# Merge and branch products of a hybrid diffusion layer: token halves as the standing operand, 512 weight columns as the moving one

## The chip, the cores and the metric

One NeuronCore of one Trainium2 chip. The metric is device time of one execution in microseconds, lower is better. Engines: TensorE (PE, with weight loads PEld), VectorE (DVE), ScalarE (ACT), GpSimd (POOL) and SyncE (SP), which here issues all DMA.

## What is computed

One layer over 256 latent tokens (D = 2048) with 256 context tokens. After modulation and a first RMSNorm, one input projection feeds two mixers and two gates; the part at issue is the merge that follows them:

```
y   = sigmoid(gate_a) * (att @ w_branch_attn) + sigmoid(gate_r) * (rec @ w_branch_rec)
x   = x + g1 * (y @ w_out)
x   = x + g2 * conv_ffn(modulate(x, norm2_w, sh2, sc2), ...)
out = rms_norm(x, final_norm_w)
```

`gate_a` and `gate_r` (256 x 2048 each) are the last 4096 columns of the input projection `h @ w_in`. `att` (256 x 1024) is the differential attention's result. `rec = rms_norm(o, w) * silu(g)` (256 x 1024) is that of a bidirectional gated recurrence over 8 heads. All is float32.

## The kernel before

**Precision.** A float32 product is made of three products in a rounded format (fp32r): each operand is split into a high part and the rest, and high x high, high x rest and rest x high are added in PSUM. An activation is kept as a pair [high, rest]; a weight is split when it comes in.

**Weights.** `stage()` (line 65) loads a unit of 128 partitions x 1024 floats into `raw` (4 buffers), ScalarE copies it to `whi`, VectorE subtracts to `wlo` (3 buffers each). `gemm2` (line 132) lets a 128 x 128 weight tile stand and the tokens pass: one matmul of 512 columns (high and rest of 256 tokens) against the high weight, one of 256 columns against the low weight. The result, channels on partitions, has two halves in PSUM, which `fold()` (line 141) adds: a ScalarE copy and a VectorE addition. The earlier input tiles with context go through `gemm` (line 110), three matmuls of 512.

**Background.** The modulation's remaining columns (64 tiles x 2 halves, "wm") are loaded by `background()` into the same `raw` buffers and consumed by VectorE (line 345). One is taken from the list every so many ticks: each weight unit of `gemm2` is one tick, of `gemm` two, and `bg_rate` gives loads a tick: 0.5 and 0.7 in the attention, 0.1 in the recurrence, 0.55 in the merge and after. A load is consumed when the next one is issued. At the recurrence's begin all but 64 are issued.

**Flows.** Attention heads and recurrence heads are generators that a tick moves on, so that their small matmuls and transposes stand between weight units. In the recurrence one flow runs at a time (`depth[0] = 1`).

**Order.** First stage (to about 145 us): modulation and norm, with the first seven input tiles. Attention (to about 412). Recurrence (to about 800): at each head, projections, their preparation on all engines, then `start(head(...))`. At head 0 the gates of channel tiles 0 and 1 follow (8 units). Then 8 tiles of the output gate `RG`, the rest of the flows, and `rec`.

**Merge.** For each of 16 channel tiles j: the two gates of tile j + 2 (4 units, PSUM from `acc`, 3 banks), the attention branch (1 unit) and the recurrence branch (1 unit, PSUM `macc`, 4 banks), each with a fold. GpSimd multiplies gates, VectorE multiplies and adds, and ScalarE and VectorE split `y` into its pair (lines 720 and 721). The recurrence's row statistic `rrstd` is a 128 x 256 tile, equal on all partitions.

**Output projection.** 16 tiles of 2 units; tiles 0 and 1 interleave, first the units with y tiles 0 to 7, then those with 8 to 15. The residual follows each tile.

**Planner.** The Tile framework orders each engine's instructions ahead of time, from the program's order as a priority and its own costs; so an instruction can stand far from its place in the program. Weight splits have a raised priority. Buffers of one tag rotate; a load waits until its buffer is let go.

Of the kernel before, what the change touches and what calls it, by code (L numbers as in the profile page):

```python
# [8 lines left out]
F32 = mybir.dt.float32  # L9
# [15 lines left out]
GROUP0 = [AK, AV, AK + 1, AV + 1, RFF, RFB, RI]  # L25
NB = 10
C1 = 3
# [13 lines left out]
@with_exitstack  # L41
def body(ctx, tc, cst_d, sel_d, cb_d, ccol_d, wn_d, xT_d, xc_d, lam_d, rope_d, mask_d, wm_d, wg0_d, win_d, wba_d,
         wbr_d, wout_d, wu0_d, wup_d, wdn_d, out_d):
    nc = tc.nc
# [87 lines left out]
    def gemm2(tiles_, xs):  # L132
# [6 lines left out]
        assert all(k == len(xs) for k in ks)  # L139

    def fold(dst, ps):
        act.copy(dst, ps[:, :T])
        dve.tensor_add(dst, dst, ps[:, T:])
# [4 lines left out]
    sel = cpool.tile([P, 2], F32, name="sel")  # L148
    cb = [big.tile([P, 1024], F32, tag="x1", name=f"cb{i}", bufs=4) for i in range(2)]

# [4 lines left out]
    with ExitStack() as es:  # L155
# [139 lines left out]

        sg = big.tile([P, 1024], F32, tag="x1", name="sg", bufs=4)
        for i in range(2):
# [23 lines left out]

    def gates(j, dst):
        for i, base in enumerate((GA, GR)):
            ps = in_tile(base + j)
            fold(dst[:, i], ps)
            act.activation(dst[:, i], dst[:, i], AF.Sigmoid)
        return [dst[:, 0], dst[:, 1]]

    bg = [(t, half) for half in range(2) for t in range(32, 96)]

    with ExitStack() as esa:
# [19 lines left out]
        with ExitStack() as es:  # L351
# [5 lines left out]
            ls = at.tile([P, 6], F32, name="ls")  # L357
            lj = at.tile([P, 64], F32, name="lj")
            lamt = at.tile([P, 256], F32, name="lamt")
            dma.dma_start(lamt, lam_d)  # L360
            for i in range(2):
# [19 lines left out]
            def head(h, kT, vr, qT):  # L381
# [60 lines left out]
                pe.matmul(ops[:, 1], ones, osq, start=True, stop=True)  # L442
                rs = at.tile([P, 2, T], F32, tag="rs", name="rs")
                act.activation(rs[:, 0], ops[:, 1], AF.Sqrt, bias=epst, scale=1.0 / P)
                dve.reciprocal(rs[:, 1], rs[:, 0])
                dve.scalar_tensor_tensor(o, o, subw, rs[:, 1], op0=ALU.mult, op1=ALU.mult)
                a = big.tile([P, 2, T], F32R, tag="ar", name=f"att{h}", bufs=16)
# [37 lines left out]

        rraw = [big.tile([P, 4, T], F32, tag="x1", name=f"rraw{i}", bufs=4) for i in range(2)]
        rrstd = cpool.tile([P, T], F32, name="rrstd")
        with ExitStack() as es:
# [29 lines left out]
            def head(h, kkq, kc, PL, PC, vr):  # L518
# [35 lines left out]

                yield 1
                tp = rps.tile([P, 4, P], F32, tag="aux", name="tp", bufs=2)
# [56 lines left out]
            background(max(0, len(bg) - 64))  # L613
            g01 = big.tile([P, 2, 2, T], F32, tag="x1", name="g01", bufs=4)
            depth[0] = 1
            bg_rate[0] = BG_REC
            for h in range(8):
# [53 lines left out]
            act.activation(rrstd, s2, AF.Sqrt, bias=epst, scale=1.0 / 1024)  # L671
            dve.reciprocal(rrstd, rrstd)
# [17 lines left out]
    def residual_load(i):  # L690
        t_ = big.tile([P, 4, T], F32, tag="x1", name=f"x1_{i}", bufs=4)
        dma.dma_start(t_, xT_d[:, 4 * i:4 * i + 4])
        x1.append(t_)
# [4 lines left out]

    residual_load(0)
    residual_load(1)  # L700
    bg_rate[0] = BG_MRG
    y = []
    for j in range(KT):
        gs = pre[j]
        if j + 2 < KT:
            pre.append(gates(j + 2, et.tile([P, 2, T], F32, tag="gate", name="gate", bufs=3)))
        pa = acc5()
        gemm2([(pa, [(wba_d[j], 1024)])], att)
        t1 = et.tile([P, T], F32, tag="e2", name="t1", bufs=4)
        fold(t1, pa)  # L710
        pool.tensor_tensor(gs[0], t1, gs[0], ALU.mult)
        pool.tensor_tensor(gs[1], rrstd, gs[1], ALU.mult)
        pr = acc5()
        gemm2([(pr, [(wbr_d[j], 1024)])], rec)
        t2 = et.tile([P, T], F32, tag="e2", name="t2", bufs=4)
        fold(t2, pr)
        dve.tensor_mul(t2, t2, gs[1])
        dve.tensor_add(t2, t2, gs[0])
        yy = et.tile([P, 2, T], F32R, tag="y", name=f"y{j}", bufs=16)
        act.copy(yy[:, 0], t2)  # L720
        dve.tensor_sub(yy[:, 1], t2, yy[:, 0].bitcast(F32))
        y.append(yy)

# [27 lines left out]
    mod_sum(32, 48)  # L751
    residual_load(2)
    sqs = et.tile([P, T], F32, tag="sqs", name="sqs2")
# [58 lines left out]
    for j in range(FT):  # L812
# [35 lines left out]
        else:  # L848
            fj = et.tile([P, 2, T], F32R, tag="y", name=f"f{j}", bufs=16)
        act.copy(fj[:, 0], sg)  # L850
# [32 lines left out]

_INS = ["cst", "sel", "cb", "ccol", "wn", "xT", "xc", "lam", "rope", "mask", "wm", "wg0", "win", "wba", "wbr", "wout", "wu0", "wup", "wdn"]


def _layout(np, x, c, ctx, c_ctx, w_mod, b_mod, norm1_w, w_in, lam_q1, lam_k1, lam_q2, lam_k2, subln_w, rec_lb,
# [10 lines left out]
    def halves(w):  # L898
        t = tiles(w)
        return np.ascontiguousarray(t.reshape(t.shape[0], P, 2, 1024).transpose(0, 2, 1, 3))  # L900

    lam = np.concatenate([A["lam_q1"][0], A["lam_k1"][0], A["lam_q2"][0], A["lam_k2"][0]])
# [13 lines left out]
    def tok(a):  # L916
# [21 lines left out]
               xc=np.concatenate([tok(A["x"]), tok(A["ctx"])], axis=2), lam=np.broadcast_to(lam, (P, 256)), rope=rope, mask=mask, wm=wm, wg0=g0,  # L938
               win=halves(wi), wba=tiles(A["w_branch_attn"][0]), wbr=tiles(A["w_branch_rec"][0]),
               wout=halves(A["w_out"][0]), wup=halves(A["w_up"][0]), wdn=tiles(A["w_down"][0]))  # L940
# [21 lines left out]
```

## Time and profile before

| | |
|---|---|
| three runs, us | 1902.01, 1905.36, 1903.25 (median 1903.25) |
| the profiled execution, us | 1907.5, its span 1905.7 |
| mean granted TensorE clock | 0.993 of full speed |
| busy share: PE, PEld, DVE, ACT, POOL | 97%, 82%, 71%, 52%, 19% |

The span is from the first to the last instruction of the profiled execution; the runs are timed without a profile. Busy shares are means over stages with different limits. A matmul's duration in the profile is its passage through a pipeline; what it costs in a stream is the distance from its start to the next one's.

### The profile page before, as it was taken

Reading aid. Unit: us, or ns where it says so; the run is one execution under the profiler, and the core shown is the slowest. Engines: PE = TensorE matmul, PEld = TensorE weight load, DVE = VectorE, ACT = ScalarE, POOL = GpSimd, SP = SyncE. Lnnn points to the kernel's source line nnn. Section 1 sums busy time; section 2 is a strip of 40 time slices with the busy share of each in tenths; the row PEclk is TensorE's granted clock in tenths of the full one; section 3 lists DMA queues with packets and bytes.
Section 4 is the critical chain, followed back from the end, with each engine's and each line's share of the span. In section 5 each row is a group of like instructions: output and inputs, shape, how many; then the busy total and the mean of one; then the engine's idle time right before and its main releaser. Section 6 shows DMA issues by size and latency. Waiting matters only on the chain.

```text
span 1905.7 us, 27947 instructions
## 1 busy us (share of the span) xinstructions
PE 1846.0 (97%) x10430; PEld 1559.7 (82%) x10430; DVE 1359.8 (71%) x2130; ACT 996.9 (52%) x1503; POOL 367.6 (19%) x328
## 2 busy tenths in 40 slices
PE   7999999998999999999999999999999999999997
PEld 3777778777788888888888789888888888888886
DVE  4449888888866667977877879776777767644444
ACT  3336455447655556744444556655555555544342
POOL 0002100003232333410110120322223222211111
PEclk9999999999999999999999999999999999999999
DMA  9977666684233333688888866666666666666664
GB/s 375 362 272 231 205 198 205 211 274 133 78 110 111 114 108 113 209 271 279 274 271 272 266 190 181 189 192 189 188 193 189 193 188 188 188 188 189 193 192 123
DMA packets 112360, 385.71 MB, mean 202 GB/s; under 512 B 12384, under 2 KB 16608, under 8 KB 112224
## 3 DMA queue, kind: packets, MB, share of 16 engines
q1 hardware_dynamic: 112224, 383.92, 63.5%
q8 instruction: 82, 1.34, 0.3%
q14 instruction: 54, 0.44, 0.1%
HBM read 381.78 MB, written 2.10 MB: 201 GB/s over the span
## 4 chain that ended last, share of the span: by engine, by line
PE 63%; DMA 9%; DVE 8%; issue 3%; ACT 2%; POOL 0%; DVEq 0%; ACTq 0%; POOLq 0%
PE macc L126 28%; PE macc L127 15%; DMA raw<-in_wm 9%; PE acc L126 5%; PE acc L77 3%; PE acc L78 3%; PE acc L79 3%; DVE wlo L73 3%; PE acc L127 2%; DVE raw L345 1%; PE lv L590 1%; ACT whi L72 1%; DMA raw<-in_win 0%; DVE PL L643 0%; PE stp L581 0%
## 5 line engine op out<-in xcount | busy, mean ns | idle before, releaser
L73 DVE TENSOR_TENSOR wlo<-raw,whi 128x1024 fp32r<-128x1024 f32 (+1 forms) x514 | 630.6, 1227 | 247.9 <-ACT whi L72 242.1
L72 ACT CAST whi<-raw 128x1024 fp32r<-128x1024 f32 (+1 forms) x514 | 530.3, 1033 | 443.4 <-PE macc L126 162.0
L126 PE MATMUL macc<-h,whi 128*128 128x512 f32 x1344 | 466.0, 391 | 0.0
L127 PE MATMUL macc<-h,wlo 128*128 128x256 f32 x1344 | 376.3, 280 | 0.0
L126 PE MATMUL acc<-h,whi 128*128 128x512 f32 x896 | 321.6, 400 | 0.0
L126 PEld LDWEIGHTS macc<-h,whi 128*128 128x128 f32 x1344 | 251.3, 187 | 55.1
L127 PE MATMUL acc<-h,wlo 128*128 128x256 f32 x896 | 253.7, 283 | 4.9 <-DVE wlo L73 4.7
L127 PEld LDWEIGHTS macc<-h,wlo 128*128 128x128 f32 x1344 | 254.0, 189 | 0.0
L126 PE MATMUL macc<-f,whi 128*128 128x512 f32 x704 | 244.1, 391 | 0.0
L77 PE MATMUL acc<-h,whi 128*128 128x512 f32 x528 | 211.4, 400 | 0.0
L79 PE MATMUL acc<-h,wlo 128*128 128x512 f32 x528 | 207.0, 392 | 0.7 <-DVE wlo L73 0.7
L78 PE MATMUL acc<-h,whi 128*128 128x512 f32 x528 | 207.3, 393 | 0.0
L345 DVE SCALAR_TENSOR_TENSOR raw<-raw,cb 128x1024 f32<-128x1024 f32 x128 | 162.7, 1272 | 61.8 <-DMA raw<-in_wm 61.4
L126 PEld LDWEIGHTS acc<-h,whi 128*128 128x128 f32 x896 | 169.3, 189 | 37.5 <-ACT whi L72 0.4
L127 PE MATMUL macc<-f,wlo 128*128 128x256 f32 x704 | 197.1, 280 | 0.0
L127 PEld LDWEIGHTS acc<-h,wlo 128*128 128x128 f32 x896 | 170.1, 190 | 11.5 <-DVE wlo L73 11.1
L126 PEld LDWEIGHTS macc<-f,whi 128*128 128x128 f32 x704 | 131.6, 187 | 28.9
L127 PEld LDWEIGHTS macc<-f,wlo 128*128 128x128 f32 x704 | 133.1, 189 | 0.0
L842 POOL TENSOR_TENSOR u<-u 128x256 f32<-128x256 f32 x44 | 69.3, 1574 | 327.9 <-DVE u L837 287.9
L79 PEld LDWEIGHTS acc<-h,wlo 128*128 128x128 f32 x528 | 99.3, 188 | 22.4 <-DVE wlo L73 1.2
L78 PEld LDWEIGHTS acc<-h,whi 128*128 128x128 f32 x528 | 99.6, 189 | 21.5 <-issue 2.8
L77 PEld LDWEIGHTS acc<-h,whi 128*128 128x128 f32 x528 | 99.4, 188 | 21.2 <-issue 2.3
(740 smaller groups left out, 2639.3 us busy)
## 6 DMA issues: line engine op xcount, KB each, us to landing
raw<-in_win SPq DMA_DIRECT2D x178, 512.0 KB, 4.2
raw<-in_wup SPq DMA_DIRECT2D x168, 512.0 KB, 3.5
raw<-in_wm SPq DMA_DIRECT2D x128, 512.0 KB, 4.4
raw<-in_wdn SPq DMA_DIRECT2D x80, 512.0 KB, 3.7
nraw<-in_wn SPq DMA_DIRECT2D x64, 512.0 KB, 7.2
raw<-in_wout SPq DMA_DIRECT2D x32, 512.0 KB, 3.6
raw<-in_wba SPq DMA_DIRECT2D x16, 512.0 KB, 4.6
raw<-in_wbr SPq DMA_DIRECT2D x16, 512.0 KB, 4.6
```

The lines of the kernel that those rows point to most:

```text
L72: act.copy(hi[:, :n], raw[:, :n])
L73: dve.tensor_sub(lo[:, :n], raw[:, :n], hi[:, :n].bitcast(F32))
L77: pe.matmul(ps, wh, xh, start=first, stop=False)
L78: pe.matmul(ps, wh, xl, start=False, stop=False)
L79: pe.matmul(ps, wl, xh, start=False, stop=last)
L126: pe.matmul(ps, hi[:, c_], xs[k][:, :, :T], start=k == 0, stop=False)
L127: pe.matmul(ps[:, :T], lo[:, c_], xs[k][:, 0, :T], start=False, stop=k == len(xs) - 1)
L345: dve.scalar_tensor_tensor(raw, raw, 1.0, cb[half], op0=ALU.mult, op1=ALU.mult, accum_out=modp[:, t - 32, half:half + 1])
L590: pe.matmul(lvp[:, m], E[:, 0, m * P:(m + 1) * P], E[:, 1, m * P:(m + 1) * P], start=True, stop=True)
L842: pool.tensor_tensor(cs[1], cs[0], cs[1], ALU.mult)
```

## The change

The gates and both branch products go to a new `gemmx`: halves of the tokens (128 each) stand, 512 weight columns pass, so the result has tokens on partitions and 512 channels in a bank. High and rest add up in the same bank, and `fold` isn't needed. A group g of 512 channels takes 8 units for each gate and 4 for each branch; the weights are laid out for it on the host (`wide`). `rrstd` becomes a column of two numbers per partition. The sums are turned back to channels on partitions by transposes in a flow (`turn`). Both gates of group 0 are made at head 0 of the recurrence (16 units, PSUM from the 3 banks of `acc`), and the attention branch of group 0 right behind the recurrence's flows. The output projection interleaves four tiles at its start. Residual loads stand behind the merge loop. Some buffers change count or tag (`x1` 5, `nraw` 9, the `RG` tile shares `sq`).

```diff
-NB = 10
+NB = 9
...
+    def gemmx(pss, units, xs, k=0):
+        for src in units:
+            hi, lo = stage(src, 1024)
+            for i in range(2):
+                c_ = slice(i * 512, (i + 1) * 512)
+                for m in range(2):
+                    t_ = slice(m * P, (m + 1) * P)
+                    pe.matmul(pss[m], xs[k][:, 0, t_], hi[:, c_], start=k == 0, stop=False)
+                    pe.matmul(pss[m], xs[k][:, 1, t_], hi[:, c_], start=False, stop=False)
+                for m in range(2):
+                    t_ = slice(m * P, (m + 1) * P)
+                    pe.matmul(pss[m], xs[k][:, 0, t_], lo[:, c_], start=False, stop=k == len(xs) - 1)
+                k += 1
+            tick(1)
...
-    def gates(j, dst):
-        for i, base in enumerate((GA, GR)):
-            ps = in_tile(base + j)
-            fold(dst[:, i], ps)
-            act.activation(dst[:, i], dst[:, i], AF.Sigmoid)
-        return [dst[:, 0], dst[:, 1]]
+    def acc3():
+        return acc.tile([P, 512], F32, tag="acc", name="acc")
+
+    def gate(i, g, accs):
+        pss = [accs() for _ in range(2)]
+        gemmx(pss, [wgt_d[i, g, u] for u in range(8)], hx)
+        dst = big.tile([P, 2, 512], F32, tag="x1", name="gate", bufs=5)
+        for m in range(2):
+            act.activation(dst[:, m], pss[m], AF.Sigmoid)
+        return dst
+
+    def branch_att(ga, g, accs):
+        pa = [accs() for _ in range(2)]
+        gemmx(pa, [wbr_d[0, g, u] for u in range(4)], att)
+        for m in range(2):
+            dve.tensor_mul(ga[:, m], pa[m], ga[:, m])
...
-        rrstd = cpool.tile([P, T], F32, name="rrstd")
+        rrstd = cpool.tile([P, 2], F32, name="rrstd")
...
-                yield 1
+                yield 4 if h == 0 else 1
...
-                    pre = [gates(j, g01[:, j]) for j in range(2)]
+                    pre = [gate(i, 0, acc3) for i in range(2)]
...
-                t_ = rt.tile([P, T], F32, tag="rg", name="rg")
+                t_ = rt.tile([P, T], F32, tag="sq", name="rg")
...
             drain()
+            branch_att(pre[0], 0, acc3)
             sp = rps.tile([P, 4, P], F32, tag="aux", name="sp", bufs=2)
-            s2 = sp[:, 0:2].rearrange("p a b -> p (a b)")
-            pe.matmul(s2, ones, sqacc, start=True, stop=False)
-            pe.matmul(s2, ones, sqlast, start=False, stop=True)
+            for m in range(2):
+                t_ = slice(m * P, (m + 1) * P)
+                pe.matmul(sp[:, m, 0:2], sqacc[:, t_], ones[:, 0:2], start=True, stop=False)
+                pe.matmul(sp[:, m, 0:2], sqlast[:, t_], ones[:, 0:2], start=False, stop=True)
...
-    residual_load(0)
-    residual_load(1)
     bg_rate[0] = BG_MRG
     y = []
-    for j in range(KT):
-        gs = pre[j]
-        if j + 2 < KT:
-            pre.append(gates(j + 2, et.tile([P, 2, T], F32, tag="gate", name="gate", bufs=3)))
-        pa = acc5()
-        gemm2([(pa, [(wba_d[j], 1024)])], att)
...
+    def turn(yy, ty):
+        yield 2
+        for m in range(2):
+            t_ = slice(m * P, (m + 1) * P)
+            tp = acc.tile([P, 4, P], F32, tag="acc", name="tp")
+            for i in range(4):
+                pe.transpose(tp[:, i], ty[:, m, i * P:(i + 1) * P], ident)
+            act.copy(yy[:, :, 0, t_], tp)
+            dve.tensor_sub(yy[:, :, 1, t_], tp, yy[:, :, 0, t_].bitcast(F32))
+            yield 1
+
+    for g in range(4):
+        ga, gr = pre if g == 0 else [gate(i, g, acc5) for i in range(2)]
+        if g:
+            branch_att(ga, g, acc5)
+        pr = [acc5() for _ in range(2)]
+        gemmx(pr, [wbr_d[1, g, u] for u in range(4)], rec)
+        for m in range(2):
+            dve.scalar_tensor_tensor(gr[:, m], pr[m], rrstd[:, m:m + 1], gr[:, m], op0=ALU.mult, op1=ALU.mult)
+            dve.tensor_add(gr[:, m], gr[:, m], ga[:, m])
+        yy = et.tile([P, 4, 2, T], F32R, tag="y", name=f"y{g}", bufs=4)
+        start(turn(yy, gr))
+        y += [yy[:, i] for i in range(4)]
+    for i in range(3):
+        residual_load(i)
...
-    residual_load(2)
...
     for j in range(KT):
-        if j % 2 == 0:
-            pair = [(acc5(), [(wout_d[j + i, 0], 1024), (wout_d[j + i, 1], 1024)]) for i in range(2)]
+        if j % 4 == 0:
+            four = [(acc5(), [(wout_d[j + i, 0], 1024), (wout_d[j + i, 1], 1024)]) for i in range(4)]
             if j == 0:
-                gemm2(pair, y)
-        if j > 1:
-            gemm2([pair[j % 2]], y)
-        ps = pair[j % 2][0]
+                gemm2(four, y)
+                drain()
+        if j > 3:
+            gemm2([four[j % 4]], y)
+        ps = four[j % 4][0]
```

## Rows read from the trace of the kernel before

**Rows 1.** The page: busy time, share of the span and instructions of each engine.
```profile
PE 1846.0 (97%) x10430; PEld 1559.7 (82%) x10430; DVE 1359.8 (71%) x2130; ACT 996.9 (52%) x1503; POOL 367.6 (19%) x328
```

**Rows 2.** Busy us (and instructions) by stretch; clock, DMA share, GB/s.
```profile
812.00:1063.00 251.00, 242.83 (x1340) 205.59 (x1339) 194.49 (x276) 116.63 (x185) 26.83 (x29) 0.99 0.84 273
...
1063.00:1080.00 17.00, 14.78 (x76) 12.56 (x75) 15.16 (x26) 7.88 (x11) 0.90 (x2) 0.90 0.83 272
...
1080.00:1100.00 20.00, 20.00 (x117) 17.50 (x116) 17.84 (x30) 11.49 (x23) 4.30 (x4) 1.00 0.78 248
```

**Rows 3.** TensorE's list, eight pairs from start to start (start, duration, line).
```profile
901.00 0.39 PE L126 MATMUL macc<-att,whi 128*128 128x512 f32 x1
...
903.78 0.39 PE L126 MATMUL macc<-rec,whi 128*128 128x512 f32 x1
```

**Rows 4.** TensorE's list: the merge's first gate matmul.
```profile
800.27 0.58 PE L126 MATMUL acc<-h,whi 128*128 128x512 f32 x1
```

**Rows 5.** Line 126: min/median/max ns, first and last start.
```profile
L126 PEld LDWEIGHTS macc<-y,whi x256: 187/188/335, 1063.3 to 1155.8; 128*128 128x128 f32 x128
...
L126 PE MATMUL macc<-y,whi x256: 391/395/796, 1063.4 to 1156.0; 128*128 128x512 f32 x128
```

**Rows 6.** Waits in the merge, SyncE's queue last: us, times, longest.
```profile
PEld acc L127 <- DVE wlo L73: 10.0, 19, 1.1
...
DVE raw L345 <- DMA raw<-in_wm: 30.5, 39, 2.8
...
SPq L341 <- DVE raw L345: 60.2, 32, 4.1
```

**Rows 7.** The chain that ended last, in the merge, shares by line.
```profile
by line: DMA raw<-in_wm 45.8%; issue 14.8%; PE acc L126 8.7%; DVE wlo L73 7.2%; PE macc L126 6.7%; PE acc L127 4.9%; PE macc L127 3.7%; DVE raw L345 2.8%; ACT whi L72 2.5%; DMA raw<-in_wba 1.8%; DVE gate L143 0.7%; DVE t L717 0.6%; DVE t L1
```

**Rows 8.** TensorE's list, a stream of 512-wide matmuls, 21 steps.
```profile
505.67 0.39 PE L79 MATMUL acc<-h,wlo 128*128 128x512 f32 x1
...
510.44 0.39 PE L79 MATMUL acc<-h,wlo 128*128 128x512 f32 x1
```

**Rows 9.** Stretch 812 to 1063: tile raw (VectorE, ScalarE), then line 345 (VectorE).
```profile
812.00:1063.00 251.00, 162.03 (x176) 88.37 (x85) 0.99 0.84 273
...
812.00:1063.00 251.00, 60.08 (x92) 0.99 0.84 273
```

**Rows 10.** Groups of the attention stage: busy us, mean ns of one.
```profile
L415 DVE SCALAR_TENSOR_TENSOR p<-p,z 128x512 f32<-128x512 f32 x16 | 12.1, 753 | 0.1
...
L424 DVE TENSOR_TENSOR aT<-tp,aT 128x512 fp32r<-128x512 f32 x16 | 10.4, 679 | 0.0
...
L423 ACT CAST aT<-tp 128x512 fp32r<-128x512 f32 x16 | 9.4, 587 | 8.5 <-PE tp L421 8.4
```

**Rows 11.** TensorE's list around four transposes.
```profile
420.93 0.60 PE L558 MATMUL tp<-ident,g0sb 128*128 128x128 f32 x4
...
421.29 0.48 PE L126 MATMUL acc<-h,whi 128*128 128x512 f32 x1
```

**Rows 12.** TensorE's waits at the output projection's start.
```profile
PE macc L126 <- DVE y L721: 2.2, 1, 2.2
```

**Rows 13.** ScalarE's list: one table load.
```profile
810.06 1.28 ACT L326 ACT_TABLE_LOAD   x1
```

**Rows 14.** TensorE's waits at heads 0 and 1 of the recurrence.
```profile
PE ktp L565 <- issue: 3.0, 1, 3.0
...
PE ktp L565 <- DVE KQ L526: 2.6, 1, 2.6
```

**Rows 15.** SyncE's waits in the first stage.
```profile
SPq L182 <- PE nat L177: 59.0, 16, 5.0
```

**Rows 16.** SyncE's issues in the merge.
```profile
846.60 0.33 SPq L341 DMA_DIRECT2D raw<-in_wm  x1
...
848.12 0.42 SPq L692 DMA_DIRECT2D x<-in_xT  x1
...
865.09 0.33 SPq L341 DMA_DIRECT2D raw<-in_wm  x1
```

More of the change, by code (lines that the diff above doesn't have):

```diff
@@ L41, in body @@
 @with_exitstack
-def body(ctx, tc, cst_d, sel_d, cb_d, ccol_d, wn_d, xT_d, xc_d, lam_d, rope_d, mask_d, wm_d, wg0_d, win_d, wba_d,
-         wbr_d, wout_d, wu0_d, wup_d, wdn_d, out_d):
+def body(ctx, tc, cst_d, sel_d, cb_d, ccol_d, wn_d, xT_d, xc_d, lam_d, rope_d, mask_d, wm_d, wg0_d, win_d, wgt_d, wbr_d,
+         wout_d, wu0_d, wup_d, wdn_d, out_d):
     nc = tc.nc
@@ L139, in gemm2 @@
         assert all(k == len(xs) for k in ks)
+    def gemmx(pss, units, xs, k=0):
[12 more added lines that the diff above has]
+            tick(1)
+        assert k == len(xs)
     def fold(dst, ps):
@@ L148, in body @@
     sel = cpool.tile([P, 2], F32, name="sel")
-    cb = [big.tile([P, 1024], F32, tag="x1", name=f"cb{i}", bufs=4) for i in range(2)]
+    cb = [big.tile([P, 1024], F32, tag="x1", name=f"cb{i}", bufs=5) for i in range(2)]
     hx = [None] * KT
@@ L294, in body @@
             g0raw[GROUP0[i]] = r
-        sg = big.tile([P, 1024], F32, tag="x1", name="sg", bufs=4)
+        sg = big.tile([P, 1024], F32, tag="x1", name="sg", bufs=5)
         for i in range(2):
@@ L357, in body @@
             ls = at.tile([P, 6], F32, name="ls")
-            lj = at.tile([P, 64], F32, name="lj")
-            lamt = at.tile([P, 256], F32, name="lamt")
-            dma.dma_start(lamt, lam_d)
+            lamt = big.tile([P, 320], F32, tag="ar", name="lamt", bufs=16)
+            lj = lamt[:, 256:]
+            dma.dma_start(lamt[:, :256], lam_d)
             for i in range(2):
@@ L442, in head @@
                 pe.matmul(ops[:, 1], ones, osq, start=True, stop=True)
[L443 to L446, printed above, removed]
+                rs = at.tile([P, T], F32, tag="rs", name="rs")
+                act.activation(rs, ops[:, 1], AF.Sqrt, bias=epst, scale=1.0 / P)
+                dve.reciprocal(rs, rs)
+                dve.scalar_tensor_tensor(o, o, subw, rs, op0=ALU.mult, op1=ALU.mult)
                 a = big.tile([P, 2, T], F32R, tag="ar", name=f"att{h}", bufs=16)
@@ L483, in body @@
             drain()
-        rraw = [big.tile([P, 4, T], F32, tag="x1", name=f"rraw{i}", bufs=4) for i in range(2)]
-        rrstd = cpool.tile([P, T], F32, name="rrstd")
+        rraw = [big.tile([P, 4, T], F32, tag="x1", name=f"rraw{i}", bufs=5) for i in range(2)]
+        rrstd = cpool.tile([P, 2], F32, name="rrstd")
         with ExitStack() as es:
@@ L613, in body @@
             background(max(0, len(bg) - 64))
-            g01 = big.tile([P, 2, 2, T], F32, tag="x1", name="g01", bufs=4)
             depth[0] = 1
@@ L690, in residual_load @@
     def residual_load(i):
-        t_ = big.tile([P, 4, T], F32, tag="x1", name=f"x1_{i}", bufs=4)
+        t_ = big.tile([P, 4, T], F32, tag="x1", name=f"x1_{i}", bufs=5)
         dma.dma_start(t_, xT_d[:, 4 * i:4 * i + 4])
@@ L697, in mod_sum @@
         dve.tensor_add(modv[:, a:b], modv[:, a:b], col("bmod", a, b - a))
-    residual_load(0)
-    residual_load(1)
     bg_rate[0] = BG_MRG
     y = []
-    for j in range(KT):
-        gs = pre[j]
-        if j + 2 < KT:
-            pre.append(gates(j + 2, et.tile([P, 2, T], F32, tag="gate", name="gate", bufs=3)))
-        pa = acc5()
-        gemm2([(pa, [(wba_d[j], 1024)])], att)
[L709 to L722, printed above, removed]
+    def turn(yy, ty):
[22 more added lines that the diff above has]
+        residual_load(i)
     warm = et.tile([P, 1], F32, name="warm")
@@ L848, in body @@
         else:
-            fj = et.tile([P, 2, T], F32R, tag="y", name=f"f{j}", bufs=16)
+            if j % 4 == 0:
+                fp = et.tile([P, 4, 2, T], F32R, tag="y", name=f"f{j}", bufs=4)
+            fj = fp[:, j % 4]
         act.copy(fj[:, 0], sg)
@@ L881, in body @@
             finish(dve, 2, c_)
-_INS = ["cst", "sel", "cb", "ccol", "wn", "xT", "xc", "lam", "rope", "mask", "wm", "wg0", "win", "wba", "wbr", "wout", "wu0", "wup", "wdn"]
+_INS = ["cst", "sel", "cb", "ccol", "wn", "xT", "xc", "lam", "rope", "mask", "wm", "wg0", "win", "wgt", "wbr", "wout", "wu0", "wup", "wdn"]
 def _layout(np, x, c, ctx, c_ctx, w_mod, b_mod, norm1_w, w_in, lam_q1, lam_k1, lam_q2, lam_k2, subln_w, rec_lb,
@@ L900, in halves, with wide @@
         return np.ascontiguousarray(t.reshape(t.shape[0], P, 2, 1024).transpose(0, 2, 1, 3))
+    def wide(w):
+        k, n = w.shape
+        return w.reshape(k // 256, 2, P, n // 512, 512).transpose(3, 0, 2, 1, 4).reshape(n // 512, k // 256, P, 1024)
     lam = np.concatenate([A["lam_q1"][0], A["lam_k1"][0], A["lam_q2"][0], A["lam_k2"][0]])
@@ L938, in _layout @@
                xc=np.concatenate([tok(A["x"]), tok(A["ctx"])], axis=2), lam=np.broadcast_to(lam, (P, 256)), rope=rope, mask=mask, wm=wm, wg0=g0,
-               win=halves(wi), wba=tiles(A["w_branch_attn"][0]), wbr=tiles(A["w_branch_rec"][0]),
+               win=halves(wi[:, :GA * P]),
+               wgt=np.stack([wide(wi[:, b * P:(b + 16) * P]) for b in (GA, GR)]),
+               wbr=np.stack([wide(A["w_branch_attn"][0]), wide(A["w_branch_rec"][0])]),
                wout=halves(A["w_out"][0]), wup=halves(A["w_up"][0]), wdn=tiles(A["w_down"][0]))
```

2 lines of the change are left out of this document (1 added, 1 removed).

## The prediction

> **What bounds the kernel now.** I read the engine line of the page first: TensorE has work for 97% of the span, and VectorE is next with 71% [rows 1]. The busy time by stage then shows where that average hides something: in the merge (812 to 1063 us) VectorE is busy 194 of 251 us and TensorE is not full [rows 2]. So the question is what a weight unit (1024 columns of a weight tile per partition) costs there, against what TensorE alone needs. In a clean stretch of the instruction list a pair of matmuls, 512 and then 256 columns, recurs 8 times in 2.78 us, 0.3475 us each [rows 3]; that is one unit. The merge runs 88 units (14 channel tiles × 2 gates × 2, and 32 for the branches) between its first gate matmul [rows 4] and the first output-projection matmul [rows 5]: 1063.4 − 800.3 = 263.1 us, 2.99 us a unit. So 0.21 us of each unit, 18 us in all, is not TensorE's.
>
> Who takes it? The list of waits says that TensorE stands for the low half of a weight [rows 6], that VectorE stands idle for a modulation transfer (wm) on 39 occasions, and that SyncE holds the next wm load until VectorE has finished the one before. The chain inside the merge runs 45.8% through those transfers [rows 7]. So the four raw buffers set the pace there: a load lands, VectorE consumes it, the buffer goes to the next load.
>
> **The change, part by part.** *The product on TensorE.* Per 256 rows of depth and 512 output channels it was 8 pairs, and is 12 matmuls of 512 columns: the same columns. In a stretch of 512-wide matmuls 21 steps take 4.77 us, 0.227 us each [rows 8], so a unit needs 12 × 0.227 = 2.73 us in place of 2.78. The gain is small, for in the pair the 256-wide one costs 0.3475 − 0.227 = 0.12 us, about half. The Trainium skill, Perfetto Trace Analysis, Optimizing Tensor Performance, says that larger matmuls are more efficient than smaller ones. TensorE: Matmul & The Clock Gate, Back-to-back issue gap, gives about 131 ns for N=512 and 81 ns for N=128 in a stream; an estimate by interpolation from that page, 98 ns for 256, makes 8 pairs 1.83 us and twelve wide ones 1.57 us, 0.26 us a unit instead of 0.05, 25 us over 96 units. The trace doesn't agree: 227 ns [rows 8], not 131.
>
> *Where the units run.* 20 units stand outside the merge loop now (16 for the first two gates, 4 for the first attention branch, beside the recurrence or right behind it, where few wm loads come), 76 inside; it was 8 and 88. Before: 8 × 2.78 + 263.1 = 285.3 us. After: 20 × 2.73 + 76 r. If the raw buffers don't hold TensorE any more, r is 2.73 and the sum 262.1 (−23.2). If they hold it as now, r is 2.99 and the sum 281.8 (−3.5). For the first: the low half is needed after four matmuls (0.91 us), no longer after one (0.23 us), and the waits for it are mostly short; VectorE loses the folds and products, all that it did outside the raw tile, 194.5 − 162.0 = 32.5 us [rows 2, 9], and gets 30 operations of 512 columns at 0.68 to 0.75 us [rows 10], 21 us. ScalarE and GpSimd lose work too. For the second: 39 of 46 times VectorE waited for the transfer itself [rows 6, 9], and a shorter queue on VectorE makes no transfer land sooner. I take the middle, r = 2.86: 54.6 + 217.4 = 272.0, **−13.3 us**.
>
> *Modulation loads pushed on.* 64 are left when the recurrence begins. At 0.1 a tick and 112 ticks, then 0.55 and 88, 4 were left for the output projection; with 124 ticks and then 76, 10 are. Six more stand beside the first residuals, where VectorE is already busy 33.0 of 37 us [rows 2]. At the merge's price, 0.21 × 1.82 units = 0.38 us each, **+2.3**; bounds 0 (hidden) and 6 × 1.31 = 7.8, a full consumption each [rows 9].
>
> *Transposes.* 32 new ones in 8 sets of four. A set of the recurrence takes 0.36 us of TensorE's list [rows 11]: **+2.9**. They stand two and three ticks behind the product, where their sources are long done, save for the last group.
>
> *The boundary to the output projection.* The wait of 2.2 us for the last y [rows 12] goes, since four tiles' first halves (8 to 11 us) need only the first two groups. Late next is the last group's second set: its transposes come three units in, 8.2 us, then a ScalarE copy (0.59) and a VectorE subtraction (0.68) [rows 10] with their queues, against a need after 4 units and 4 pairs, 12.5 us. About a microsecond is left, so **−1.5**, bounds −2.2 and +2.
>
> *PSUM banks of the early gates.* Each holds two of three banks for 8 units; the second gate's second bank waits until the first gate's sigmoid has left it. From rows: the tail of a matmul 0.39 [rows 3], a table load 1.28 [rows 13], a 512-wide ScalarE pass 0.59 [rows 10], less the two matmuls ahead, 0.45: 1.8 us of TensorE, and 0 if the planner fills it with the recurrence. I take **+1**. The Trainium skill, Perfetto Trace Analysis, Optimizing Tensor Performance, speaks against this part: independent groups should rotate through different banks, so that leaving one overlaps the next group. By that rule the whole 1.8 counts and the sum is 0.8 us worse; no run here shows such a gate yet.
>
> *The recurrence.* The head of the flow waits four ticks and the second gate's units lie between heads 0 and 1. There TensorE stood 3.0 and 2.6 us for transposes that were placed ahead of their source [rows 14], because two heads' preparation met on VectorE. With 22 us of product between them it should meet less: **−2**, bounds −5.6 (both go) and +5.6 (as much again).
>
> *Taken at nothing.* The row statistic, two products of 256 columns, becomes four of two columns. Nine first-stage buffers for ten: SyncE's loads wait there for TensorE to free a buffer, 59 us in 16 waits [rows 15], and none of TensorE's waits is for them; uncovered, one load would come one slot later, once, 1 to 2 us. The recurrence-gate tile shares a buffer with a head's key sum; three product banks cover its delay. The three residual loads behind the loop could block SyncE's weight loads, some 7 us (landing, copy, subtraction), but the planner has put such a load amid the merge's weights already, 45 us past its place in the program [rows 16].
>
> Sum: −13.3 + 2.3 + 2.9 − 1.5 + 1 − 2 = −10.6. The profiled execution took 1907.5 us (span 1905.7, 1.8 around it), so it would take 1896.9. The median of the runs shown is 1903.25, 4.25 below the profiled one; there −10.6 gives **1892.7**.
>
> **Rivals.** *The buffers let go entirely.* r = 2.73, the rest as above: −23.2 + 2.7 = −20.5, 1882.8. For it speak the short waits for the low half, against it the chain [rows 7].
>
> *Nothing comes of it in the merge.* r = 2.99: −3.5 + 2.7 = −0.8, 1902.5. That is the change not doing what it does on VectorE, because a landing and not a queue is waited for. TensorE's shorter unit is then waited away.
>
> *Slower: the wm loads fall into single file.* If each is issued only when the one before is consumed, as in three successive steps of 6.16 us (846.60 to 865.09) [rows 16], the loop sets the pace and TensorE's own need doesn't matter. The merge's mean now is 251 / 46 = 5.46 us [rows 9], since some overlap. A different plan of buffers may lose that. Halfway, 5.8 us for 42 loads is 243.6 us: 54.6 + 243.6 = 298.2, +12.9 + 2.7 = +15.6, 1918.9. It decides from about 5.6 us a load on; below, the change is not slower. For it: 32 SyncE waits of this kind now [rows 6]; against: the same program order of loads.
>
> *Wide matmuls run at the pace of their weight loads.* At 0.188 us a load [rows 5] a unit would take 12 × 0.188 = 2.26 us; in the 20 units outside the merge that is 9.4 us more gained, inside it the buffers would still hold: −10.6 − 9.4 = −20.0, 1883.3. The 512-wide stream of now, a load before each matmul, speaks against it at 0.227 [rows 8]. The rule on larger matmuls in the Trainium skill, Perfetto Trace Analysis, Optimizing Tensor Performance, would count for more in this case.
>
> **How the numbers follow.** The forecast (r from 2.80 to 2.93, 1887 to 1898) gets 0.42, the buffers letting go 0.18, nothing in the merge 0.23, single file 0.15, the weight loads' pace 0.02. A measurement of this kernel tells changes from about 0.2%, 3.8 us: faster is below 1899.4, slower above 1907.1. Nearly all of the first two is faster, of the third a quarter (the others' bounds, some −4 to −7), with six tenths in between; single file is slower. Faster 0.64, same 0.17, slower 0.19. The range reaches from 1880 (the second case, with the recurrence's waits half gone) to 1909 (the third with the modulation loads' upper bound, +5.5, and a microsecond more); outside are most of single file and a little below, under 0.2.
>
> **What would show it.** In the profile after: a unit of product 2.73 us apart in clean stretches, and 76 units in the merge over about 217 us; waits of TensorE for the low half fewer, SyncE's waits for VectorE's wm step still there; VectorE's time outside raw tiles down by a third; wm steps until some 50 us into the output projection; no wait of 2 us at its start; the heads' 3.0 and 2.6 us shorter. The prediction is wrong if wm loads stand further apart than 5.5 us, if TensorE waits for a bank or for transposes at the early gates, or if weights for the output projection are late behind the residual loads.

## The result and the profile after

The changed kernel is slower: 1932.13 us (median of 4 runs, 1926.45 to 1935.38) against 1902.63 for the kernel before, a ratio of 1.0145 with the 95% interval 1.0124 to 1.0165. The prediction said 1892.7, with a range of 1880 to 1909. The profiled execution took 1935.38 us, its span 1933.6, 27.9 more than that of before.

The page's engine line, beside [rows 1]:

```profile
PE 1846.3 (95%) x10082; PEld 1550.5 (80%) x10082; DVE 1339.5 (69%) x2050; ACT 972.7 (50%) x1410; POOL 344.0 (18%) x296
```

TensorE's busy time is what it was (1846.0), and every other engine does less. So the added time is idle time of TensorE (and some slow time: the same instructions take 1831.0 us busy in experiment 1 below), and a table by stage says where. Each stage runs from the first matmul of one to the first of the next; the gates that moved from the merge into the recurrence are taken out of both with 8 × 2.73 = 21.8 us.

| stage, us | before | after | difference without the moved gates |
|---|---|---|---|
| start to the end of attention | 410.9 | 412.6 | +1.7 |
| recurrence, with the early gates (8, then 16 units) | 389.4 | 443.8 | +32.6 |
| merge, up to the output projection (88, then 80 units) | 263.1 | 232.0 | −9.3 |
| output projection | 93.2 | 94.9 | +1.7 |

The row statistic stands at the end of the recurrence before (798.40 to 800.27) and in the merge after, so some 2 us belong to the other row. Differences of 2 us in a stage are within what two profiles of one kernel differ by (the attention ends at 408.5 and 406.6 us in the two of experiment 1).

The merge gained about what was forecast. The recurrence lost three and a half times that. TensorE's waits of the changed kernel from 400 to 880 us (us in all, times, longest) name one line:

```profile
PE ktp L594 <- DVE KQ L555: 32.6, 7, 6.0
PE lv L619 <- ACT E L578: 2.0, 1, 2.0
PE macc L150 <- ACT rrstd L702: 1.7, 1, 1.7
```

Line 594 (565 before) transposes KQ, the last piece of a head's preparation. Before, these transposes waited at heads 0 and 1 alone [rows 14]. Now they wait at each of heads 1 to 7, 4.7 us on average. TensorE's list of the changed kernel at one head (start, duration, line):

```profile
646.40 0.60 PE L587 MATMUL tp<-ident,vr 128*128 128x128 f32 x4
651.54 1.11 PE L594 MATMUL ktp<-ident,KQ 128*128 128x128 f32 x4 [4.54 <-DVE KQ L555]
652.30 0.78 PE L77 MATMUL acc<-h,whi 128*128 128x512 f32 x1
652.88 0.63 PE L78 MATMUL acc<-h,whi 128*128 128x512 f32 x1
653.30 0.63 PE L79 MATMUL acc<-h,wlo 128*128 128x512 f32 x1
...
657.10 0.39 PE L79 MATMUL acc<-h,wlo 128*128 128x512 f32 x1
```

Behind the wait stand weight products (lines 77 to 79) that need nothing of KQ: the transposes come first in TensorE's list, so the products are held up with them. They also run slower at first, 0.42 us from start to start (652.88 to 653.30) and not 0.227 [rows 8], up to 657.10. The windows round an earlier head's wait show the granted clock (PE, PEld, DVE, ACT, POOL busy, PEclk, DMA share, GB/s):

```profile
594.00:599.40 5.40, 0.90 (x7) 0.54 (x5) 5.37 (x6) 1.64 (x5) 4.49 (x5) 0.96 0.10 39
599.40:607.00 7.60, 7.57 (x30) 6.31 (x31) 6.69 (x17) 4.53 (x9) 1.26 (x2) 0.80 0.24 69
607.00:639.00 32.00, 32.00 (x172) 27.52 (x172) 17.69 (x34) 13.59 (x18) 5.83 (x6) 1.00 0.37 115
```

First TensorE stands (0.90 us of 5.40 busy), then it has work without a gap at 0.80 of the full clock, and then at 1.00. Up to 602.46, where the matmuls run 0.42 us apart, the clock is 0.51, the lower level of 1.2 GHz. Set against the same number of instructions in experiment 1 below, what follows the wait takes 1.5 us longer at this head, 2.6 at the one listed before, 1.2 to 2.6 at heads 1 to 6 and 0.1 at head 7, some 11 us in all beyond the waits. The Trainium skill, TensorE: Matmul & The Clock Gate, "Wait — 56ns, not 53.3ns?", gives 426.7 ns from start to start for 512 columns on a cold array; the trace agrees (420 to 430).

### The profile page after: what moved, and what is told of

Its sections match the earlier page's. It is cut to its first block, busy times and chain, and to the rows that moved or that the text cites. A ratio compares the mean times of both kernels' runs of the same rounds, so it can differ in the third digit from the quotient of the medians.

```text
span 1933.6 us, 27041 instructions
## 1 busy us (share of the span) xinstructions
PE 1846.3 (95%) x10082; PEld 1550.5 (80%) x10082; DVE 1339.5 (69%) x2050; ACT 972.7 (50%) x1410; POOL 344.0 (18%) x296
## 3 DMA queue, kind: packets, MB, share of 16 engines
q1 hardware_dynamic: 112224, 383.92, 61.9%
## 4 chain that ended last, share of the span: by engine, by line
PE 69%; DVE 11%; DMA 10%; issue 4%; ACT 4%; POOL 2%; DVEq 0%; SPq 0%; ACTq 0%; POOLq 0%
PE macc L126 27%; PE macc L127 14%; DMA raw<-in_wm 8%; DVE wlo L73 3%; PE acc L126 3%; PE acc L77 3%; PE acc L78 3%; PE acc L79 3%; PE g L195 2%; PE acc L195 2%; PE nat L195 2%; DVE raw L374 2%; PE acc L127 1%; ACT whi L72 1%; DVE PL L671 1%
## 5 line engine op out<-in xcount | busy, mean ns | idle before, releaser
L73 DVE TENSOR_TENSOR wlo<-raw,whi 128x1024 fp32r<-128x1024 f32 (+1 forms) x514 | 623.6, 1214 | 218.1 <-ACT whi L72 211.6
L77 PE MATMUL acc<-h,whi 128*128 128x512 f32 x528 | 215.0, 407 | 0.0
L78 PE MATMUL acc<-h,whi 128*128 128x512 f32 x528 | 211.2, 400 | 0.0
L126 PE MATMUL acc<-h,whi 128*128 128x512 f32 x384 | 139.2, 403 | 0.0
L775 POOL TENSOR_TENSOR sqs<-sqs,sq 128x256 f32<-128x256 f32 x28 | 35.7, 1275 | 485.1 <-ACT sq L774 485.1
L78 PEld LDWEIGHTS acc<-h,whi 128*128 128x128 f32 x528 | 101.8, 193 | 22.7 <-issue 3.2
L79 PEld LDWEIGHTS acc<-h,wlo 128*128 128x128 f32 x528 | 101.7, 193 | 22.5 <-issue 1.0
L77 PEld LDWEIGHTS acc<-h,whi 128*128 128x128 f32 x528 | 102.0, 193 | 21.9 <-issue 2.1
L127 PE MATMUL acc<-h,wlo 128*128 128x256 f32 x384 | 107.7, 280 | 0.9 <-DVE wlo L73 0.8
L126 PE MATMUL macc<-y,whi 128*128 128x512 f32 x256 | 90.8, 399 | 2.3 <-DVE y L742 2.3
```

The costliest lines, as they stand in the source:

```text
L73: dve.tensor_sub(lo[:, :n], raw[:, :n], hi[:, :n].bitcast(F32))
L77: pe.matmul(ps, wh, xh, start=first, stop=False)
L78: pe.matmul(ps, wh, xl, start=False, stop=False)
L79: pe.matmul(ps, wl, xh, start=False, stop=last)
L126: pe.matmul(ps, hi[:, c_], xs[k][:, :, :T], start=k == 0, stop=False)
L127: pe.matmul(ps[:, :T], lo[:, c_], xs[k][:, 0, :T], start=False, stop=k == len(xs) - 1)
```

## The theory

*Theory A: the place in ticks.* In the recurrence one flow moves at a time. A head's flow that starts while the one before still runs stands in the queue, and its transposes come that much later. Counted from the program, before: from head 0's start to head 1's are 10 ticks (8 gate units, 2 of RQ), and head 0's flow needs 14. So head 1 starts 4 ticks late, and since every later head brings 14 ticks of product and its flow takes 13 or 14, moved on by units of one or two, all later heads stay 4 ticks late. From the end of the product RQ, which begins the preparation's last part, to the transposes of KQ it is 10 ticks at heads 2 to 6.

The change gives 18 ticks (16 gate units), and with its `yield 4` head 0's flow needs 17. Head 1 now starts on time, and so do all after it: 6 ticks in place of 10. The preparation doesn't get shorter with that. In the changed kernel it takes from 628.38 (ScalarE's copy of RQ) to 651.5 (the end of KQ), 23.1 us, and the transposes stand at 647.0. It even gets longer, as the last section shows. Head 7, with 7 ticks by the same count, waits 2.5 us, the least of the seven.

*The rival:* the heads wait because VectorE has more to do there, the early gates' staging and modulation loads, whatever the ticks.

## The experiments

**1. The lag put back.** In the changed kernel:

```
-                yield 4 if h == 0 else 1
+                yield 8 if h == 0 else 1
```

Head 0's flow now needs 21 ticks, so head 1 starts late again: 10 ticks from RQ to KQ's transposes, with no other change of the work.

> The changed kernel with one number altered: head 0's flow waits 8 ticks at its start, not 4, so that head 1's flow again starts late and every later head's key transposes (ktp) stand 10 ticks behind the head's last prepared product, as in the kernel before, and not 6. Theory A (the position of the transposes in TensorE's order is too early for the preparation of KQ): TensorE's waits at ktp fall from 32.6 us to under 6, the time from 1932 to 1895 to 1908. Rival B (the 16 gate units and their wide drains beside the recurrence slow the preparation itself, wherever the transposes stand): the waits stay above 20 us, the time above 1922.

1886.29 us (1884.36 to 1890.23), ratio to before 0.9911 (0.9883 to 0.9938): faster than theory A's range, and than the kernel before. Its engine line, TensorE's waits from 400 to 822 us and TensorE's list at the head that answers to the one above:

```profile
PE 1831.0 (97%) x10082; PEld 1539.3 (82%) x10082; DVE 1324.5 (70%) x2050; ACT 971.9 (52%) x1412; POOL 339.9 (18%) x296
```

```profile
PE lv L619 <- DVE S L622: 1.6, 1, 1.6
PE macc L150 <- ACT rrstd L702: 1.5, 1, 1.5
PE acc L126 <- DVE rg L161: 1.1, 1, 1.1
PE ktp L594 <- issue: 0.8, 1, 0.8
```

```profile
633.57 0.60 PE L587 MATMUL tp<-ident,vr 128*128 128x128 f32 x4
634.00 0.60 PE L594 MATMUL ktp<-ident,KQ 128*128 128x128 f32 x4
634.36 0.48 PE L77 MATMUL acc<-h,whi 128*128 128x512 f32 x1
```

The waits for KQ are gone. The preparation still needs its time: RQ's copy starts at 602.90 and the scans end at 621.1, 18.2 us later, 2.8 less than in the changed kernel (628.38 to 649.4). KQ ends at 629.3 (628.64 and 0.69), since ScalarE makes its exponents only from 627.79 on, and the transposes come at 634.0, 4.7 us after that. The recurrence takes 399.9 us, 43.9 less than in the changed kernel: 31.8 are the waits at line 594, some 11 the slow stretches behind them. It is 11 us shorter than before without the moved gates (399.9 − 21.8 = 378.1 against 389.4). Of that some 2 are the row statistic and 4.8 the waits at heads 0 and 1 [rows 14], 5.6 before and 0.8 now; before, the clock from 454 to 500 us, round these waits, is 0.89, and in experiment 1 it is 1.00 over the whole stage. Why these two waits went is open: head 0 has 10 ticks for 3, but head 1 has 8 in both, and in experiment 2 head 0 waits 0.8 us with 3.

**2. The kernel before, with the lag taken away.** Four ticks let pass with nothing in them, behind head 0's gates:

```
                     pre = [gates(j, g01[:, j]) for j in range(2)]
+                    tick(4)
```

> The kernel before with nothing of the change but its phase: four empty ticks after head 0's gates, which let head 0's flow end before head 1's begins, so that ktp stands 6 ticks behind the product and not 10. Theory A: five to seven waits of 4 to 6 us at ktp appear in the recurrence, the time goes from 1903 to 1922 to 1940. Rival B: no such waits, 1899 to 1908.

1941.22 us (1938.65 to 1945.22), ratio 1.0201 (1.0177 to 1.0224). The wait of the changed kernel is there without any of the change, in as many places:

```profile
PE ktp L565 <- DVE KQ L526: 29.8, 7, 5.5
```

The recurrence takes 428.4 us, 39 more than before; the merge 263.1, as before. So the place in ticks makes the loss without any of the change's work, and the rival falls as its cause. The time is a little above the range expected, since the flow's other products waited too (7.4 us in 6 waits at the level products, line 590).

**3. Half the lag,** `yield 6`: 8 ticks from RQ.

> The changed kernel with a wait of 6 ticks at head 0: ktp stands 8 ticks behind the product, about 24 us of matmuls, against a preparation that ends some 24 us after it in the changed kernel. Theory A: waits at ktp between 0 and 1.5 us a head, 0 to 10 us in all, time 1895 to 1912. Rival B: above 20 us of waits, above 1922.

1896.74 us in a single run, and one wait for KQ:

```profile
PE ktp L594 <- DVE KQ L555: 3.4, 1, 3.4
```

It stands at head 1, which has 6 ticks by the count. Heads 2 to 7 have 8 and wait for KQ nowhere, so two ticks more are enough there. The recurrence takes 408.4 us; the waits and slow steps behind them that the trace shows make part of the 8.5 above experiment 1.

**4. No gates beside the recurrence:** `yield 1`, and `pre = [gate(i, 0, acc3) for i in range(2)]` moved behind `drain()`. With no units between heads 0 and 1 the lag at heads 2 to 6 grows to 18 ticks.

> The changed kernel with the two gates of group 0 taken away from head 0 (they stand behind the recurrence's flows instead), and head 0's wait at 1 tick. ktp then stands 16 to 18 ticks behind the product and the last head's flow has 9 ticks left when the products end. Theory A: no waits at ktp; the tail can stand among the 16 gate units; 1897 to 1915. Rival B: fast as well, since the gates are no longer beside the recurrence; so this run tells only together with the first.

1917.61 us in a single run, slower than expected. TensorE's waits from 400 to 860 us:

```profile
PE lv L619 <- DVE S L622: 11.4, 5, 3.3
PE lv L619 <- DVE E L581: 8.6, 3, 7.5
PE ktp L594 <- issue: 3.8, 1, 3.8
```

No head waits for KQ, but the level products do, for VectorE's masked copies (S) and exponents (E): a flow that is so late meets the next head's preparation there, as I read the releasers. So the expectation, that a longer lag is always enough, was wrong: with 6, 8, 10 and 18 ticks the times are 1932.1, 1896.7, 1886.3 and 1917.6, the best of these at 10. The last differs in a second thing, the gates taken from between heads 0 and 1; 8.6 and 3.8 of these waits lie there, and only the 11.4 at later heads speak for the lag.

**5. What the merge gained from: the low half needed later?** Experiment 1 with each token half taking its low-weight product second of three, so that the low half is needed after one matmul and not after four:

```
                     pe.matmul(pss[m], xs[k][:, 0, t_], hi[:, c_], start=k == 0, stop=False)
-                    pe.matmul(pss[m], xs[k][:, 1, t_], hi[:, c_], start=False, stop=False)
-                for m in range(2):
-                    t_ = slice(m * P, (m + 1) * P)
-                    pe.matmul(pss[m], xs[k][:, 0, t_], lo[:, c_], start=False, stop=k == len(xs) - 1)
+                    pe.matmul(pss[m], xs[k][:, 0, t_], lo[:, c_], start=False, stop=False)
+                    pe.matmul(pss[m], xs[k][:, 1, t_], hi[:, c_], start=False, stop=k == len(xs) - 1)
```

> The lag-8 version with another order inside the wide product: for each token half high x high, then low weight x high, then high weight x rest, so that the low half of a weight is needed after one matmul (0.23 us) and not after four (0.91 us). Theory L (the merge gained because the low half is needed later): the stretch from the first recurrence-branch matmul of the merge to the first output-projection matmul, 217.7 us with lag 8, grows by 5 us or more, the time from 1886 to 1891 or more. Rival D (it gained because VectorE, ScalarE and GpSimd have less beside the staging): 215 to 221 us, time 1883 to 1889.

1889.9 us (1887.47 to 1895.35), and the merge loop takes 217.7 us, the same as in experiment 1. That reason falls. The time is 0.9 above what rival D gave; ahead of the merge TensorE waits 2.7 us for the first early gate's sigmoid to leave a bank here, against 0.7 in experiment 1.

**6. From the modulation loads?** The kernel before with `BG_REC` at 0.5 for 0.1, which moves the wm loads from the merge into the recurrence.

> The kernel before with 0.5 modulation loads a tick in the recurrence in place of 0.1, so that all of them are consumed there and none stands beside the merge. Theory S (the 0.21 us a unit of the merge before comes from these loads in the four raw buffers): its 88 units take 244 to 250 us, not 263; the recurrence, whose VectorE gets some 50 more consumptions of 1.3 us, becomes longer by 5 to 40 us. Rival (the folds and products on VectorE and GpSimd hold the merge by themselves): 257 us or more. The total is expected between 1895 and 1930, for it adds up both.

1924.68 us, ratio 1.0107 (1.0083 to 1.0131). The merge falls from 263.1 to 249.2 us, 2.83 a unit: of the 0.21 us a unit that were not TensorE's [rows 2 to 5], the wm loads made 0.16. But the recurrence grows by 33.4, with TensorE's waits

```profile
PE lv L590 <- DVE S L593: 13.8, 5, 4.1
PE ktp L565 <- DVE KQ L526: 6.3, 4, 2.3
```

so the loads are cheaper in the merge than there. The 6.3 us at line 565, at unchanged ticks, show that more work on VectorE can also make the transposes wait, though not 30 us of it.

**7. From the work taken off VectorE, ScalarE and GpSimd?** Experiment 1 with such work put back, in operations on scratch tiles that nothing reads: a fold's ScalarE copy and VectorE addition of 256 columns behind every second unit of the merge loop (the first), or a GpSimd product of 256 columns behind every third (the second).

```
+            nu[0] += 1
+            if nu[0] % 2:
+                act.copy(du[0], ones[:, 0:1].broadcast_to([P, T]))
+                dve.tensor_add(du[1], du[1], du[0])
```

```
+            if nu[0] % 3 == 1:
+                pool.tensor_tensor(du[2], du[2], du[1], ALU.mult)
```

> The lag-8 version with idle work put back beside the merge: behind every second weight unit a ScalarE copy and a VectorE addition of 256 columns on a scratch tile, so that both engines carry per unit about what the folds cost before (VectorE 0.39 us a unit outside the raw tile, now 0.20; ScalarE 0.34, now 0.15). Nothing of the result depends on it. Theory D (less work beside the staging is what the merge gained beyond the 0.05 us a unit of the wide matmuls): the stretch from the first recurrence-branch matmul to the first output-projection matmul grows from 217.7 us by 3 to 6. Rival: 217 to 219, and the gain stays unexplained.

> The lag-8 version with a GpSimd product of 256 columns on a scratch tile behind every third weight unit of the merge, the 0.32 us a unit of GpSimd that the merge before had and the changed one lacks. Theory P (GpSimd's work slowed the staging): the same stretch grows from 217.7 us by 3 or more, VectorE's low-half subtraction gets longer than 1.22 us on average. Rival: 217 to 219.

Single runs, read by the stage: the loop takes 221.1 us with the folds and 225.6 with GpSimd's products, against 217.7 and 215.2 in two profiles without. So the folds cost 3.3 to 5.9, little more than the 2.5 by which those two differ, and GpSimd's products 7.9 to 10.4, though no GpSimd instruction stands in the chain of that stretch. More GpSimd time was put back than the merge before had, 32.9 us in 225.6 against 26.8 in 251 [rows 2], so the price is rather an upper one. The products lengthen VectorE's subtraction, by 76 × 0.058 = 4.4 us in all; how the rest comes about is not shown. The groups of line 73 in the merge loop (count, busy us, mean ns; idle before), with GpSimd's products and in experiment 1:

```profile
L73 DVE TENSOR_TENSOR wlo<-raw,whi 128x1024 fp32r<-128x1024 f32 x76 | 97.3, 1280 | 21.1 <-ACT whi L72 20.8
```

```profile
L73 DVE TENSOR_TENSOR wlo<-raw,whi 128x1024 fp32r<-128x1024 f32 x76 | 92.8, 1222 | 17.1 <-ACT whi L72 17.1
```

**8. More from the merge?** Experiment 1 with the transposes of the first three groups later, `yield 2 if g == 3 else 4`: first with the row statistic ahead of the attention branch, then that with `BG_REC` 0.3 as well, then alone, beside a second run of experiment 1.

> The lag-8 version with the turning transposes of groups 0 to 2 two ticks later, and the row statistic ahead of the first attention branch. If each wait that TensorE shows there is worth its length: the 3.1 us for the transposes and the 1.5 us for the statistic's bank go, 1880 to 1883. Rival (the raw buffers hold the merge, so that a wait removed turns up again as one for a weight's low half): 1885 to 1888, with waits for the low half up by 3 us or more.

> The version with later transposes and 0.3 modulation loads a tick in the recurrence in place of 0.1, so about 25 of the 52 that stood beside the merge and output projection go to the recurrence, where the transfer queues are emptier. Theory S: the merge and output projection lose most of their waits for weights, 4 to 8 us; if the recurrence takes the loads in its gaps, 1874 to 1881; if its heads wait for VectorE instead, 1884 to 1900.

> The lag-8 version with the turning transposes of groups 0 to 2 two ticks later, and the row statistic left where it was: the 3 us of waits for transposes go without the 1.7 us that the moved statistic cost ahead of the merge. 1881 to 1885, against the lag-8 version 1.5 to 4 us less; the rival, that a wait comes back elsewhere: no difference.

> The lag-8 version once more, on the same chip as the one with later transposes, for the comparison: 1883 to 1890, before 1900 to 1906.

The first gave 1887.29 us (ratio 0.9916, 0.9898 to 0.9934), the rival's time, though the weight loads' waits for the low half rose by 1.3 us only (5.5 to 6.8), the second 1904.04 (0.9997, 0.9982 to 1.0012), above either of its ranges. The second's loop takes 212.5 us, 2.1 less than the first's, and its recurrence 425.8, 25.9 more than experiment 1's. The third gave 1886.97 (0.9918, 0.9898 to 0.9939), slower than expected, the repeat 1887.6 (0.9926, 0.9908 to 0.9944), as expected. The loop is 1.7 us shorter with the transposes later (213.5 against 215.2), which the time can't tell from nothing. The best version stays that of experiment 1, some 0.8% faster than the kernel before, and it beats both.

## Why the prediction was wrong

**The step that failed is "The recurrence".** It took −2 with bounds of −5.6 and +5.6 and measured +32.6. It argued that the product between heads 0 and 1 would thin out VectorE's work there, and read only the two waits that the trace showed [rows 14]. What set the other heads' transposes, how many ticks stand between a head's preparation and its use, was not counted, though the ticks were counted for the wm loads. Heads 2 to 7 showed no wait before because they were 4 ticks late, and the change took that lateness away: a cover that no list of waits shows. The bounds came from the waits on record, and so could not hold a new one at seven heads. The slow clock behind six of the seven waits, some 11 us, was in no term.

**The merge** was right in its sum. Forecast were 76 units at 2.86 with six sets of transposes, 217.4 + 6 × 0.36 = 219.5 us, and measured 218.4 (870.0 to 1088.4), in experiment 1 217.7 and 215.2. The unit of 2.73 us is there, twelve matmuls in 2.74; TensorE's list of the changed kernel:

```profile
870.34 0.40 PE L151 MATMUL macc<-whi,rec 128*128 128x512 f32 x1
...
873.08 0.39 PE L151 MATMUL macc<-whi,rec 128*128 128x512 f32 x1
```

Its make-up is another one. 76 × 2.73 = 207.5 and the transposes' 2.2 leave 8.7, and most of that are TensorE's waits in the loop, 5.4 us for transposes and 1.1 for the low half, that I had not priced; that the sum came out is partly luck. The waits of the changed kernel, the first three from 870 to 1088 us, the last at the output projection's start:

```profile
SPq L370 <- DVE raw L374: 61.9, 30, 4.0
PE tp L740 <- DVE gate L753: 5.4, 2, 5.1
PEld macc L154 <- DVE wlo L73: 1.5, 1, 1.5
...
PE macc L126 <- DVE y L742: 2.3, 1, 2.3
```

The weight loads' waits for the low half went to 1.5 us, 5.5 in experiment 1. Before, they were 10.0 at the gates [rows 6] and, at the branches, which the prediction did not read (812 to 1063 us):

```profile
PEld macc L127 <- DVE wlo L73: 7.6, 14, 2.5
```

The raw buffers still hold SyncE's wm loads as before (61.9 us in 30 waits), but that reaches TensorE little: without the 5.4 us of waits for transposes a unit costs (218.4 − 2.2 − 5.4) / 76 = 2.77 us, so the rival "the buffers let go entirely" (2.73) was nearer than the middle that I took (2.86). "Single file" did not come: 41 wm steps in 218 us are 5.3 us each. VectorE's time outside the raw tile fell by half (152.3 − 137.0 = 15.2 us of 218, against 32.5 of 251 [rows 2, 9]):

```profile
870.00:1088.00 218.00, 211.46 (x935) 174.10 (x936) 152.26 (x186) 89.36 (x95) 0.00 (x0) 0.99 0.84 281
...
870.00:1088.00 218.00, 137.02 (x157) 77.83 (x74) 0.99 0.84 281
```

Of the reasons given for it, the later need of the low half is refuted by experiment 5, and the lighter VectorE, ScalarE and GpSimd are borne out by experiment 7, for GpSimd more clearly than for the folds; GpSimd, which the prediction named in half a sentence, weighed most there. With experiment 6 the parts come to more than the 18 us they share: the wm loads cost 13.9 us beside the folds and products, and the loop without these carries 41 of them at little cost. So they act together. The prediction's 263.1 starts at the second gate matmul [rows 4]; the first stands at 798.65, ahead of the row statistic, a difference of one pair. Its border for single file is 5.5 us by its own sum, and not 5.6.

**The turn's transposes** were taken to have their sources long done "save for the last group"; one earlier set waited 5.1 us for VectorE's sum (line 753).

**The boundary.** The wait for y should have gone (−1.5); 2.3 us of 2.2 stayed, so the "about a microsecond" that was left was not there. With ten wm loads, as counted (the last 47.7 us into the stage), the output projection became 1.7 us longer, against +2.3 − 1.5 and 0.7 for two sets of transposes: close in sum, with the wait's term wrong.

**The early gates' bank** cost 0.2 us (TensorE's wait at line 150 for the first gate's sigmoid), not 1, so the 1.8 that the prediction set beside the Trainium skill's rule on rotating banks was not seen in the changed kernel. The same wait is 0.7 us in experiment 1 and 2.7 in experiment 5, so 1.8 is no upper bound either. A wait of 1.7 us for the row statistic ahead of the recurrence branch, which I had at nothing, stands instead. Nine first-stage buffers for ten: the attention ends at 412.6 us here and at 408.5 in experiment 1, against 410.9, no loss to be seen. The wide stream did not run at the pace of its weight loads (0.228 us a matmul above, not 0.188).

Without the failed step, the other terms hold in sum: experiment 1 has the whole change and no waits for KQ, and outside the recurrence its profile is 8.2 us shorter than before, against −8.6. The recurrence gave 11.3 there and not 2, which was not forecast, and that puts its 1886.3 to 1887.6 us within the range, but 5 to 6 us below the forecast.

## What to carry to other kernels

Where small dependent operations are placed into a stream of products by a count, write down for each how many units stand between its source's start and its use, before and after, above all where a change adds work at the head of a queue: a lag that carries on from item to item is a cover, and a list of waits shows nothing of it. Bounds taken from the waits that exist say nothing about waits that don't exist yet; for these take the duration of the preparation against the distance. The distance also decides what the preparation runs beside, and so how long it takes. Then tune the distance by itself, in both directions, since too late costs as well.

## What the runs showed of the hardware

VectorE's scans ran much longer beside GpSimd's work than without it. The groups of the scans at lines 671 and 673, in the changed kernel from 480 to 812 us and in experiment 1 in the same window:

```profile
L671 DVE TENSOR_TENSOR_SCAN PL<-ones,fq 128x256 f32<-128x256 f32 x21 | 21.4, 1072 | 0.0
...
L673 DVE TENSOR_TENSOR_SCAN PC<-ones,fq 128x256 f32<-128x256 f32 x14 | 18.2, 1341 | 0.0
```

```profile
L671 DVE TENSOR_TENSOR_SCAN PL<-ones,fq 128x256 f32<-128x256 f32 x21 | 12.9, 671 | 0.0
...
L673 DVE TENSOR_TENSOR_SCAN PC<-ones,fq 128x256 f32<-128x256 f32 x14 | 8.7, 665 | 0.0
```

Per head that is 3 × 0.40 + 2 × 0.68 = 2.6 us, ahead of KQ and so part of the waits of 2.5 to 6 us. In the changed kernel GpSimd runs from 590.5 us on, with the squares of the head before and the next head's key sum, and the scans run from 591.5 to 597.3. Of the 40 scans of the changed kernel's recurrence, the 7 with no GpSimd instruction beside them took 0.67 us, the other 33 1.16 in the median. The Trainium skill, SBUF — State Buffer, "SBUF: two separate sides", says that a VectorE operation with both inputs in SBUF and GpSimd's reads exclude each other; the direction agrees (671 to 1072 ns). That this overlap comes from the 4 ticks, which bring the tail of one head onto the next one's scans, experiment 2 bears out: there, with nothing but four empty ticks, the scans of the kernel before (672 and 742 ns from 480 to 812 us) become as slow (470 to 832 us):

```profile
L643 DVE TENSOR_TENSOR_SCAN PL<-ones,fq 128x256 f32<-128x256 f32 x21 | 21.4, 1072 | 0.0
L645 DVE TENSOR_TENSOR_SCAN PC<-ones,fq 128x256 f32<-128x256 f32 x14 | 17.8, 1311 | 0.0
```

So the lost ticks act in two ways, by transposes that stand earlier and by a preparation that ends later. No run parts the two; by the 2.6 us the second makes up to about half of a wait.
